# The mixer's pairs of column blocks: seven products in another order, partial sums taken from PSUM, and new constants for the recorder

## The chip, the cores and the metric

The kernel runs on one core of a Trainium2 chip. The metric is the device time of one execution in microseconds (us); for the kernel before it is 787.59 us, the median of 3 runs (787.1 to 787.76). A core has five engines that run side by side: TensorE multiplies matrices (the profile's PE, and PEld for its weight loads), VectorE (DVE) and ScalarE (ACT) do elementwise work and read the results of TensorE out of the memory called PSUM, GpSimd (POOL) does elementwise work in the other memory, SBUF, and SyncE (SP) issues most of the transfers.

## The reference

One step of a decoder layer for 512 prompt tokens and 8 x 4 sample tokens that share all weights (544 columns in all, D = 1024). Cut to what matters here:

```
h = rmsnorm(x, norm_mix);  z = h @ w_in            # the mixer's input: 28 blocks of 128 columns
aq, ak, av, hq, hf, hi, hg = split(z)              # attention q, k, v; HGRN q, forget gate, input, output gate
att = dilated_attention(aq, ak, av)                # also over cached keys and values for the samples
o   = hgrn2_recurrence(silu(hq), 1 - f, hi, log f) # f from hf; then norm, times silu(hg)
x  += concat(att, o) @ w_out
x  += cross_attention(rmsnorm(x), memory)          # memory keys and values from w_ck, w_cv
x  += (silu(conv3(u @ w_gate)) * (u @ w_up)) @ w_down,  u = rmsnorm(x)
```

All is float32. The kernel multiplies large matrices in a rounded float32 format in three passes: each operand is split into a high and a low part, and high x high, high x low and low x high are summed.

## The kernel before

Tokens lie along the free dimension (N = 544, two halves of HT = 272 columns), features along the 128 partitions. A block of 128 output features of the mixer is made either whole, by `proj_in` (8 feature tiles x 3 passes, in two cuts of 256 and 288 columns), or two blocks at once, by `proj_pair` (line 1198). The list `MIX` gives the order: h0, q0 to q3, k0, k1, then the pairs k2 with k3, v0 with v1, hf1 with hq1, hg1 with hv1 (the item `('H', 1)` makes two pairs), then the single blocks again. So `proj_pair` runs four times in a kernel. (The output projection, `wo_pair`, and the feed-forward part have pairs of their own, which the diff leaves as they are.)

A pair is Strassen's scheme in Winograd's form: the weights of two blocks are cut into A11, A12 (first block) and A21, A22 (second block), the tokens into B11, B21, B12, B22, and seven products replace eight. `take_pair` (line 861) makes the sums of weights S1 to S4, `make_blocks` the sums of tokens X, T, U, V. Each product is 12 matmuls (4 feature tiles x 3 passes) 272 columns wide. They gather in three PSUM banks: a and c come from the pool of two banks for main products ("dense"), d from the pool of five for everything else ("aux"). Bank a receives A11·B11, then S2·U, then S1·T, then S4·B22, each added onto what is there; after each of them a partial sum is read from the bank before the next product may be added.

In the kernel before the order of products is A11·B11 (a), S3·X (c), S2·U (a), A12·B21 (d), S1·T (a), S4·B22 (a), A22·V (c). ScalarE copies bank a three times: after A11·B11 into the first block's output, after S2·U and after S1·T into the two halves of an SBUF tile named `kept` (z and r). The second block's halves are then bank c minus r and bank c minus z, on VectorE (`difference`), and each half is multiplied by the row of normalisers r_mix, on VectorE too.

The order of all instructions is made by a recorder, the class `Tape` (its constants are at line 282). The kernel's functions don't issue instructions; they record steps with their reads and writes. Products under `tape.main()` form one chain whose order on TensorE is the order of recording. All else on TensorE (attention scores, HGRN blocks, the products with cached keys and values) is side work, which the recorder places between main products. It runs a model of the engines on the host, and what that model decides is the order in which each engine gets its instructions. On the chip the engines wait for each other by semaphores, so the order is fixed and the times are not. The rules that the constants set:

- Each step has a time at which it is due (`begin`), reckoned back from the steps that use it: a step that a main product needs is due `MARGIN` earlier still, and a step that nothing presses gets `SLACK` after it could start. A step on an engine other than TensorE may start up to `LEAD` ahead of its due time, unless a lead of its own is given.
- When TensorE is free and a main product is ready, a group of side work is opened if the ready side work sums to `BURST` us, or has waited for `PATIENCE` us, or is due; `NEAR` is what a change of the tile's shape counts in the choice of the next. When no main product is ready, side work runs as it comes.
- `FETCH` is the time from the asking for the next block of 256 of TensorE's instructions to its landing; side work that would run into a block not yet landed is held back. `ACTIVE` is the least share of busy time that TensorE must keep for side work to be let in.
- `EVEN` stretches the estimated times of the main chain.

In the profile nearly every instruction has line 726, the recorder's replay; so the tiles' names tell the work apart: `ps_ak`, `ps_ck`, `ps_dk` are the banks a, c, d of the first pair, `ps_av`, `ps_ahf`, `ps_ahg` bank a of the other three, `psd` and `psdo` products with cached keys and values, `psS`, `psT`, `psO` prompt attention, `psA`, `psB`, `psL`, `psin`, `psu`, `psU`, `pso` HGRN.

Of the kernel before, what the change touches and what calls it, by code (L numbers as in the profile page):

```python
# [12 lines left out]
AF = mybir.ActivationFunctionType  # L13
ALU = mybir.AluOpType
# [7 lines left out]
N = SEQ + NS  # L22
# [21 lines left out]
def ROWS_ON(nc):  # L44
    return nc.vector
# [9 lines left out]
HT = N // 2  # L55
# [218 lines left out]
class Tape:  # L274
# [4 lines left out]

    ROUNDS, EVEN = 2, 1.008
    BLOCK, AHEAD_OF, FETCH = 256, 63, 4.3
    SWITCH, NEAR = 0.16, 8.9
    SPELL, ACTIVE, IDLE, COLD = 3.4, 0.44, 0.45, 2.0
    BURST, PATIENCE, SLACK, LEAD, MARGIN = 2.05, 13.75, 14.4, 20.8, 1.3
    AHEAD = {"SP": 8, "ACT": 5, "DVE": 5, "POOL": 5, "PE": 8}

    def __init__(self, nc):
# [441 lines left out]
def tile_decoder_step(ctx: ExitStack, tc: tile.TileContext, xT, memT, kwT, vw, s0, conv_in, mkT, mv, vecs, cst,  # L731
                      w_first, w_in, w_out, w_cq, w_ck, w_cv, w_co, w_gate, w_up, w_down,
                      yT, kT_out, vT_out, st_out, conv_out, mkT_out, mv_out, ss_out):
    nc = tape = Tape(tc.nc)
# [9 lines left out]
    def A(name, shape=None, dt=F32):  # L744
        return tape.tile(act, shape or [128, FW], dt, tag="a", name=name, bufs=NA)
# [7 lines left out]
    def PD(name):  # L753
        return tape.tile(psum, [128, 512], F32, tag="dense", name=name, bufs=2)

    def PX(name):
        return tape.tile(psum, [128, 512], F32, tag="aux", name=name, bufs=5)
# [290 lines left out]
    r_mix, mix_acc = A("r_mix"), A("acc_mix")  # L1048
# [4 lines left out]
    first = [A(f"h{n}0") for n in "fqg"]  # L1053
# [109 lines left out]
    def proj_evac(out, scale, ps, n0, n):  # L1163
        if scale is None:
            nc.vector.tensor_tensor(out[:, n0:n0 + n], ps[:, :n], r_mix[:, n0:n0 + n], op=ALU.mult)
        else:
            nc.vector.scalar_tensor_tensor(out[:, n0:n0 + n], ps[:, :n], scale, r_mix[:, n0:n0 + n],
                                           op0=ALU.mult, op1=ALU.mult)
# [29 lines left out]
    def proj_pair(names):  # L1198

        name, outs = names[0], [A(n) for n in names]  # L1200
        w = ws.take_pair(name)
        a, c, d, kept = PD(f"ps_a{name}"), PD(f"ps_c{name}"), PX(f"ps_d{name}"), A(f"kept{name}")
        z, r = kept[:, :HT], kept[:, HT:N]

        def product(ps, wn, xn, first):
            with tape.main():
                for k in range(4):
                    (hi, lo), (xh, xl) = w[wn][k], mix_blocks[xn][k]
                    for i, (l, x_) in enumerate(((hi, xh), (hi, xl), (lo, xh))):
                        nc.tensor.matmul(ps[:, :HT], l, x_, start=first and k == 0 and i == 0, stop=k == 3 and i == 2,  # L1210
                                         skip_group_check=True)
            if wn not in ("S1", "S4", "A12"):
                sides.pump()

        def difference(c0, sub):
            out = outs[1][:, c0:c0 + HT]
            nc.vector.tensor_tensor(out, c[:, :HT], sub, op=ALU.subtract)
            ROWS_ON(nc).tensor_tensor(out, out, r_mix[:, c0:c0 + HT], op=ALU.mult)

        out = outs[0][:, :HT]  # L1220
        product(a, "A11", "B11", True)
        nc.scalar.copy(out, a[:, :HT])
        product(c, "S3", "X", True)
        product(a, "S2", "U", False)
        nc.scalar.copy(z, a[:, :HT])
        product(d, "A12", "B21", True)
        nc.vector.tensor_tensor(out, d[:, :HT], out, op=ALU.add)
        nc.vector.tensor_tensor(out, out, r_mix[:, :HT], op=ALU.mult)
        product(a, "S1", "T", False)
        nc.scalar.copy(r, a[:, :HT])  # L1230
        difference(HT, r)
        product(a, "S4", "B22", False)
        proj_evac(outs[0], None, a, HT, HT)
        product(c, "A22", "V", False)
        difference(0, z)
        return outs

    def proj_in(name, scale=None):
# [274 lines left out]
    mixed, outs = [None] * 8, [None] * 8  # L1513
# [199 lines left out]
    def each(kind, at, scale=None):  # L1713
        names = [f"{kind}{p}" for p in at]
        return proj_pair(names) if len(at) > 1 else [proj_in(names[0], scale)]
# [45 lines left out]
    def project_hgrn(what, h):  # L1761
        names = [f"h{n}{h}" for n in "fqg"] + [f"hv{h}"]
        if h == 0:
            f, q, gt, v = first + [proj_in(names[3])]
        elif what == "H":
            f, q, gt, v = proj_pair(names[:2]) + proj_pair(names[2:])
        else:
            f, q, gt, v = [proj_in(n) for n in names]
        hgrn(h, f, q, gt, v)
# [327 lines left out]
    hid, ups, ugs, whole, firsts, lows = {}, {}, {}, {}, {}, {}  # L2097
# [763 lines left out]
    while rest:  # L2861
        m, c = rest.pop(0)
# [81 lines left out]
```

## Time and profile before

| | |
|---|---|
| median of 3 runs | 787.59 us (787.1 to 787.76) |
| profiled execution | 786.92 us, of it 785.1 us span |
| PE busy | 774.4 us (99% of the span), 7411 matmuls |
| DVE busy | 688.9 us (88%) |
| ACT busy | 493.2 us (63%) |
| POOL busy | 216.1 us (28%) |
| mean granted TensorE clock | 0.998 |

The span runs from the first to the last instruction of the profiled execution; what its time has beyond the span lies around it. A row of the chain of waits is: start in us, duration in us, what ran (engine, tile, line, count). A row of a group of instructions is: line, engine, operation, out<-in, shapes, count | busy us, mean ns of one | idle time of the engine just before them and what ended it. A row of a stage is: the stretch, its length, then busy time and count of PE, PEld, DVE, ACT and POOL, the granted clock, the DMA engines' share and GB/s.

### The profile page before, as it was taken

To read this page: it belongs to the slowest core of one execution; us is meant where nothing else is said; L and a number is where in the kernel's file an instruction comes from. 1 tells how busy PE (TensorE), PEld (TensorE's weight loads), DVE (VectorE), ACT (ScalarE), POOL (GpSimd) and SP (SyncE) were. 2 spreads that over 40 slices of the span, in tenths; PEclk is the share of its full clock that TensorE was granted. 3 is DMA by queue.
4 is the path that set the end of the run, shared out by engine and by line. 5 is a ranking of instruction groups with operands and counts; after the bars stand their busy time and mean duration, and the time that the engine had idled before them with its cause. 6 is when DMAs were issued, how large, how long until landed. Compare 5 with 4: busy or idle time off the path is not lost.

```text
span 785.1 us, 19260 instructions
## 1 busy us (share of the span) xinstructions
PE 774.4 (99%) x7411; PEld 737.4 (94%) x7411; DVE 688.9 (88%) x1538; ACT 493.2 (63%) x1066; POOL 216.1 (28%) x298
## 2 busy tenths in 40 slices
PE   9999999999999999999999999999999999999996
PEld 8998879897899989999899999999999999999995
DVE  6899988588988989896779999999999998979983
ACT  7733467826559576574776677656665765668543
POOL 1131100031210431242234436522433242232122
PEclk9999999999999999999999999999999999999999
DMA  8745887697872776252663477887878968776303
GB/s 312 262 149 146 268 291 257 225 338 263 262 242 82 216 167 206 83 195 75 203 211 81 106 196 169 180 195 178 188 168 185 214 149 206 194 183 196 91 1 114
DMA packets 109116, 146.23 MB, mean 186 GB/s; under 512 B 7520, under 2 KB 74080, under 8 KB 109024
## 3 DMA queue, kind: packets, MB, share of 16 engines
q1 hardware_dynamic: 90992, 121.72, 47.6%
q0 software_dynamic: 17184, 22.55, 17.7%
q8 instruction: 58, 0.95, 0.5%
q10 hardware_dynamic: 848, 0.72, 0.3%
q14 instruction: 34, 0.28, 0.1%
HBM read 136.90 MB, written 8.07 MB: 185 GB/s over the span
## 4 chain that ended last, share of the span: by engine, by line
PE 95%; DVE 1%; ACT 1%; issue 1%; DMA 1%; SPq 0%; DVEq 0%
PE ps_ag L726 8%; PE ps_au L726 8%; PE ps_aw L726 5%; PE ps_cu L726 4%; PE ps_cg L726 4%; PE ps_q L726 3%; PE ps_wo L726 3%; PE ps_cq L726 3%; PE ps_dz L726 3%; PE ps_az L726 3%; PE ps_hv L726 2%; PE ps_cw L726 2%; PE ps_first L726 2%; PE ps_dg L726 2%; PE ps_du L726 2%; PE ps_ck L726 2%
## 5 line engine op out<-in xcount | busy, mean ns | idle before, releaser
L726 DVE TENSOR_TENSOR wl<-wr,wh 128x512 fp32r<-128x512 f32 x86 | 61.2, 735 | 1.5 <-ACT wh L726 1.5
L726 POOL TENSOR_TENSOR hG<-hG,hf 128x256 f32<-128x256 f32 (+1 forms) x28 | 25.5, 910 | 125.8 <-DVE hf L726 80.5
L726 ACT CAST wh<-wr 128x512 fp32r<-128x512 f32 x86 | 49.4, 616 | 5.2 <-DMA wr<-in_w_in 5.1
L726 POOL COPY last<-ug 128x2 f32<-128x2 f32 (+1 forms) x44 | 26.0, 636 | 87.4 <-DVE ug L726 80.0
L726 DVE SCALAR_TENSOR_TENSOR cv<-ug,vec,cv 128x560 f32<-128x560 f32 x44 | 35.1, 798 | 0.8 <-ACT cv L726 0.2
L726 POOL TENSOR_TENSOR acc_cx<-acc_cx,sq_cx 128x256 f32<-128x256 f32 (+1 forms) x14 | 13.9, 999 | 40.7 <-ACT sq_cx L726 40.4
L726 POOL COPY ug<-conv_state 128x16 f32<-128x16 f32 x22 | 23.6, 1138 | 0.0
L726 ACT ACTIVATE cv<-cv 128x560 f32<-128x560 f32 x22 | 14.8, 672 | 11.4 <-DVE cv L726 11.0
L726 ACT ACTIVATE cv<-ug,vec 128x560 f32<-128x560 f32 x22 | 18.9, 858 | 4.6 <-DVE ug L726 2.9
L697 POOL DMA_DIRECT2D S13w<-in_w_down x12 | 11.7, 978 | 36.3 <-DMA S13w<-in_w_down 9.0
L726 ACT ACTIVATE P<-P,mx 128x128 f32<-128x128 f32 (+3 forms) x32 | 17.6, 553 | 3.0 <-DVE mx L726 3.0
L726 PE MATMUL ps_co<-coh,wh 128*128 128x256 f32 (+1 forms) x64 | 19.2, 300 | 0.0
L726 POOL TENSOR_TENSOR acc_final<-acc_final,sq_final 128x256 f32<-128x256 f32 (+1 forms) x10 | 9.3, 942 | 35.0 <-ACT sq_final L726 18.3
L726 PE MATMUL ps_co<-col,wh 128*128 128x256 f32 (+1 forms) x64 | 18.4, 288 | 0.0
L726 PE MATMUL ps_co<-coh,wl 128*128 128x256 f32 (+1 forms) x64 | 18.4, 288 | 0.0
L697 POOL DMA_DIRECT2D A22w_0l<-in_w_down x6 | 12.2, 2042 | 18.2 <-DMA S13w<-in_w_down 7.1
L726 POOL TENSOR_TENSOR acc_ux<-acc_ux,sq_ux 128x256 f32<-128x256 f32 (+1 forms) x13 | 11.3, 873 | 21.0 <-ACT sq_ux L726 21.0
L726 POOL MEMSET hG<- 128x544 f32 x4 | 2.2, 551 | 51.7 <-PE psO L726 44.1
L726 ACT COPY keptg<-ps_ag 128x272 f32<-128x272 f32 x20 | 7.7, 385 | 13.3 <-PE ps_ag L726 13.2
L726 DVE TENSOR_TENSOR xr<-xr,ps_aw 128x272 f32<-128x272 f32 x36 | 15.5, 430 | 0.4 <-PE ps_aw L726 0.2
L726 POOL MEMSET ug<- 128x2 f32 x22 | 15.7, 763 | 0.0
L726 PE MATMUL psd<-st,qbd_win 128*32 128x224 f32 x256 | 15.7, 357 | 0.0
(3466 smaller groups left out, 3841.1 us busy)
## 6 DMA issues: line engine op xcount, KB each, us to landing
st<-in_kwT SPq DMA_DIRECT2D x32, 448.0 KB, 6.1
st<-in_vw SPq DMA_DIRECT2D x28, 512.0 KB, 6.2
wr<-in_w_in SPq DMA_DIRECT2D x25, 512.0 KB, 6.4
wrg<-in_w_gate SPq DMA_DIRECT2D x10, 512.0 KB, 6.0
wru<-in_w_up SPq DMA_DIRECT2D x10, 512.0 KB, 5.5
st<-in_mkT SPq DMA_DIRECT2D x8, 512.0 KB, 6.4
S13w<-in_w_down SPq DMA_DIRECT2D x24, 128.0 KB, 5.1
A1w<-in_w_down SPq DMA_DIRECT2D x12, 256.0 KB, 4.2
```

What stands on the lines that cost most here:

```text
L697: return tape.put(engine, lambda: call(*args, **kw), outs, ins, 0.1, 0.3, size)
L726: return tape.put(engine, lambda: call(*args, **kw), outs, ins, length, lag, size, port, codes, work, mode)
```

## The change

In `proj_pair` A22·V moves ahead of S4·B22, so the order is A11·B11 (a), S3·X (c), S2·U (a), A12·B21 (d), S1·T (a), A22·V (c), S4·B22 (a). The tile `kept` goes. ScalarE now copies bank c after S3·X into the second block's right half, and bank a, times -1, after S2·U into its left half. VectorE then takes right minus bank a after S1·T, and left plus bank c after A22·V, in place (`whole`), and multiplies by r_mix as before. The side work's generators are moved on once after the same four products as before (`sides.pump()`), so the last of these calls now comes ahead of S4·B22.

Nine of the recorder's constants get new values; its code stays.

```diff
-    ROUNDS, EVEN = 2, 1.008
-    BLOCK, AHEAD_OF, FETCH = 256, 63, 4.3
-    SWITCH, NEAR = 0.16, 8.9
-    SPELL, ACTIVE, IDLE, COLD = 3.4, 0.44, 0.45, 2.0
-    BURST, PATIENCE, SLACK, LEAD, MARGIN = 2.05, 13.75, 14.4, 20.8, 1.3
+    ROUNDS, EVEN = 2, 0.993
+    BLOCK, AHEAD_OF, FETCH = 256, 63, 5.2
+    SWITCH, NEAR = 0.16, 6.85
+    SPELL, ACTIVE, IDLE, COLD = 3.4, 0.48, 0.45, 2.0
+    BURST, PATIENCE, SLACK, LEAD, MARGIN = 1.4, 4.45, 15.85, 30.05, 3.5
...
-        a, c, d, kept = PD(f"ps_a{name}"), PD(f"ps_c{name}"), PX(f"ps_d{name}"), A(f"kept{name}")
-        z, r = kept[:, :HT], kept[:, HT:N]
+        a, c, d = PD(f"ps_a{name}"), PD(f"ps_c{name}"), PX(f"ps_d{name}")
...
-        def difference(c0, sub):
-            out = outs[1][:, c0:c0 + HT]
-            nc.vector.tensor_tensor(out, c[:, :HT], sub, op=ALU.subtract)
+        def whole(out, bank, op):
+            nc.vector.tensor_tensor(out, out, bank[:, :HT], op=op)
+            c0 = HT * (out is right)
             ROWS_ON(nc).tensor_tensor(out, out, r_mix[:, c0:c0 + HT], op=ALU.mult)
 
-        out = outs[0][:, :HT]
+        first, (left, right) = outs[0][:, :HT], (outs[1][:, :HT], outs[1][:, HT:N])
         product(a, "A11", "B11", True)
-        nc.scalar.copy(out, a[:, :HT])
+        nc.scalar.copy(first, a[:, :HT])
         product(c, "S3", "X", True)
+        nc.scalar.copy(right, c[:, :HT])
         product(a, "S2", "U", False)
-        nc.scalar.copy(z, a[:, :HT])
+        nc.scalar.activation(left, a[:, :HT], AF.Copy, scale=-1.0)
         product(d, "A12", "B21", True)
-        nc.vector.tensor_tensor(out, d[:, :HT], out, op=ALU.add)
-        nc.vector.tensor_tensor(out, out, r_mix[:, :HT], op=ALU.mult)
+        whole(first, d, ALU.add)
         product(a, "S1", "T", False)
-        nc.scalar.copy(r, a[:, :HT])
-        difference(HT, r)
+        whole(right, a, ALU.subtract)
+        product(c, "A22", "V", False)
+        whole(left, c, ALU.add)
         product(a, "S4", "B22", False)
         proj_evac(outs[0], None, a, HT, HT)
-        product(c, "A22", "V", False)
-        difference(0, z)
         return outs
```

## The prediction

> **What bounds the kernel now.** I read the page's head and busy shares first, then its chain of work that ended last, then the stages, then what the PE waits for.
>
> ```profile
> span 785.1 us, 19260 instructions
> PE 774.4 (99%) x7411; PEld 737.4 (94%) x7411; DVE 688.9 (88%) x1538; ACT 493.2 (63%) x1066; POOL 216.1 (28%) x298
> PE 95%; DVE 1%; ACT 1%; issue 1%; DMA 1%; SPq 0%; DVEq 0%
> ```
>
> The PE is busy for 99% of the span and is 95% of the chain. The busy share hides what a matmul costs, so the stages (columns: length, busy time and count for each engine, clock, DMA) say where there is room at all:
>
> ```profile
> 75.00:160.00 85.00, 84.53 (x894) 74.04 (x894) 67.06 (x188) 54.95 (x123) 5.16 (x7) 1.00 0.78 259
> 160.00:300.00 140.00, 139.13 (x1853) 122.50 (x1852) 124.65 (x328) 85.20 (x200) 35.73 (x44) 1.00 0.72 220
> 300.00:425.00 125.00, 124.54 (x1058) 119.79 (x1057) 104.41 (x215) 79.25 (x197) 38.38 (x45) 1.00 0.49 155
> 425.00:725.00 300.00, 300.00 (x2391) 299.99 (x2391) 287.87 (x591) 201.07 (x405) 110.76 (x164) 1.00 0.76 178
> ```
>
> From 425 to 725 us (the feed-forward part) the PE has no idle time, at a granted clock of 1.00; 300 us for 2391 matmuls is 125 ns each, as fast as a product of twelve gets anywhere (1.51 us, below). No new order wins there. From 75 to 425 us the PE is idle for 0.47 + 0.87 + 0.46 = 1.8 us. The waits of the PE name them (who waits, for whom, us, times, longest):
>
> ```profile
> PE ps_first L726 <- DVE zero L726: 1.1, 1, 1.1
> PE ps_ak L726 <- ACT keptk L726: 0.5, 1, 0.5
> PE psdo L726 <- ACT dom L726: 0.5, 1, 0.5
> PE ps_g L726 <- DVE xr L726: 0.5, 1, 0.5
> PE psL L726 <- ACT hAT L726: 0.3, 1, 0.3
> ```
>
> The first is the start, written in a fixed order that the diff leaves alone. The second is one of the changed pairs. So the question is small: a wait of half a microsecond, and how the side products (attention, HGRN, cached keys) are placed between the main ones, which the recorder decides.
>
> **The change part by part.** In each of the four pairs (k2 with k3, v0 with v1, hf1 with hq1, hg1 with hv1) the old order ends S1·T on bank a, S4·B22 on bank a, A22·V on bank c. S4·B22 may not start until a copy of bank a is done, and no main product lies between. The chain of waits around that place in the first pair (start, us, what):
>
> ```profile
> 89.27 1.51 PE ps_ak L726 x12
> 90.78 0.02 issue
> 90.80 0.40 ACT keptk L726
> 91.20 0.04 issue
> 91.24 1.79 PE ps_ak L726 x12
> ```
>
> The PE stands for 0.02 + 0.40 + 0.04 = 0.46 us, and the product behind it takes 1.79 instead of 1.51, 0.28 more. The new order puts A22·V, on the other bank, into that place: it takes 1.51 us and covers the release. First term: 0.46 + 0.28 = 0.74 us won.
>
> In the other three pairs the recorder filled the same hole with side products (second pair; for comparison a group of sixteen; third; fourth):
>
> ```profile
> 106.22 0.52 PE psd L726 x8
> 106.74 1.74 PE ps_av L726 x12
> ...
> 100.64 0.89 PE psd L726 x16
> ...
> 125.01 1.31 PE psT L726 x12
> ...
> 131.07 0.52 PE psd L726 x8
> 131.59 0.45 PE ps_ahf L726 x2
> ...
> 150.54 2.30 PE psdo L726 x40
> 152.84 1.71 PE ps_ahg L726 x12
> 154.55 1.51 PE ps_chg L726 x12
> ```
>
> Eight psd take 0.52 us, sixteen 0.89: eight more cost 0.37, so entering side work costs 0.52 - 0.37 = 0.15 fixed, and the main product behind it takes 1.71 instead of 1.51, another 0.20. An opening, then, costs 0.35 us beside its work. The group of eight at 106.22 stands alone only because nothing else could run; with A22·V ready it can join a later group. Second term: 0.35 us. The 2.30 us group is large enough to be opened for itself, and so is the third pair's, from 125.01 to 131.59; I count nothing for them (between nothing and 0.35 each, kept in the range).
>
> What the new order adds: bank a is now freed for S4·B22 by VectorE's subtraction (right minus a), where ScalarE's copy did it. The rows of the two operations between 75 and 160 us, and of a VectorE subtraction that reads SBUF alone:
>
> ```profile
> L726 ACT COPY keptk<-ps_ak 128x272 f32<-128x272 f32 x2 | 0.8, 388 | 1.1 <-PE ps_ak L726 1.1
> L726 DVE TENSOR_TENSOR k<-ps_ck,keptk 128x272 f32<-128x272 f32 x2 | 0.9, 432 | 0.0
> L726 DVE TENSOR_TENSOR xT<-x 128x272 f32<-128x272 f32 x4 | 1.6, 428 | 0.0
> ```
>
> Old and new have the same number of operations in a pair, three on ScalarE and seven on VectorE, all 272 wide (four of the seven read PSUM in both). The scaled copy (scale -1) has no row of its own at this width; I take the copy's 388 ns, with nothing and double that as the ends, off the path either way. So the sum of engine work is nothing, and what matters is whether VectorE comes in time. In the first pair its queue behind the end of S1·T (90.78) looked like this:
>
> ```profile
> 91.10 0.69 DVE L726 TENSOR_TENSOR S1l_v<-S_v,S1h_v 128x512 fp32r<-128x512 f32 x1
> 91.70 0.43 DVE L726 TENSOR_TENSOR k<-ps_ck,keptk 128x272 f32<-128x272 f32 x1
> ```
>
> Two 0.69 us weight splits stood before it; it ended at 92.13, 1.35 us after S1·T. With the 0.04 us of release that is 1.39, and A22·V covers 1.51. The cover holds, by 0.12 us. One more split ahead of the subtraction would cost 0.69 - 0.12 = 0.57 and the 0.28 behind a wait. I take nothing, with 0.85 us a pair as the bad end.
>
> The Trainium skill, Advanced Engine Details and Errata, The Read-Write Bubble, says that ScalarE is the engine close to PSUM and VectorE the one close to SBUF, which speaks against freeing a bank by VectorE. The trace bears it out by very little: 432 ns from PSUM against 428 from SBUF, and 388 on ScalarE, which by that rule would be 0.04 us a pair under a cover of 1.51.
>
> The end of a pair: before, bank a was free one product ahead of bank c; now c is free one product ahead of a. The next main tile finds one free bank with 1.51 us of cover in both, as at 156 us in the old trace, where the next tile follows the pair's last product without a gap. The old tile of kept halves goes, which frees one of 71 SBUF tiles: nothing, since no wait of the PE names a missing tile. In the last pass, one VectorE operation instead of two follows the last product: 0.43 us earlier, hidden under the next tile's products.
>
> **The constants** shift every step that isn't written in a fixed order. Later landing of instruction blocks (4.3 to 5.2 us) keeps side products away from block boundaries. What the profile shows of blocks (a DMA queue: packets, MB, share):
>
> ```profile
> q8 instruction: 58, 0.95, 0.5%
> ```
>
> 58 blocks of 16 KB feed the PE, and every idle stretch of the PE after the start is named above with an engine as its end, none with a block. There is nothing to win from this edit by itself. The Trainium skill, Runtime: NRT & Kernel Launch, Instruction fetch mechanics, has the next block fetched while the present one runs and the crossing mostly hidden; the trace agrees for the PE.
>
> A smaller least size for a group (2.05 to 1.4 us) and less patience (13.75 to 4.45 us) make for more openings; a longer lead (20.8 to 30.05) and an earlier due time (margin 1.3 to 3.5 us) bring work forward, which makes groups larger and takes away waits. I count 24 groups with narrow tiles in the chain from the first to the last of these rows:
>
> ```profile
> 46.67 0.75 PE psB L726 x59
> ...
> 289.16 1.64 PE pso L726 x14
> ```
>
> 24 openings at 0.35 are 8.4 us. If groups shrank with the least size there would be 24 x 2.05 / 1.4 = 35, 3.9 us more; if the work that comes forward let one in four be merged, 2.1 us less. The two pull against each other and I take nothing. The remaining waits (psdo on dom 0.5, ps_g on xr 0.5, psL on hAT 0.3, together 1.3 us) hang on one operation that came late by less than the 2.2 us by which due times move forward. The one on xr is VectorE itself standing before its work:
>
> ```profile
> 418.55 1.49 issue
> 420.05 0.45 DVE xr L726
> 420.50 0.04 issue
> ```
>
> 1.49 us in which VectorE waited for nothing that the profile shows; such a thing moves when its instructions move. I take half of the 1.3, 0.6 us, with nothing and 1.3 as the ends.
>
> **The sum.** 0.74 + 0.35 + 0.6 = 1.7 us. The profiled execution took 786.92 (span 785.1 and 1.8 around it); 786.92 - 1.7 = 785.2. The median of the runs is 787.59, 0.67 above it, and moves alike: 787.59 - 1.7 = 785.9. The three runs lie between 787.1 and 787.76; about 0.2%, 1.6 us, is what a measurement of this kernel can tell from no change, so this forecast lies at that edge.
>
> **The rivals.** First, the wins go back where they came from: the two certain terms hold (1.1 us) but new waits of the size of the old ones appear elsewhere, or VectorE is late in one pair (0.85) or three groups more are opened (1.05). For it: 24 groups are placed anew, and each wait in the list is a matter of tenths. Against it: the holes in the pairs were in all four. Time: 787.59 - 1.1 + 0.85 = 787.3, and 786.5 if nothing is given back. That the block constant does nothing at all (no stall to remove) belongs here.
>
> Second, slower: more openings. Place: between 46 and 291 us. Mechanism: a group starts at 1.4 us of ready side work or after 4.45 us, so work that filled one group is split in two. Price 0.35 us each; from 5 more openings the 1.7 us are gone, and from about 10 the kernel is slower by over 0.2%. With the full 11 worked out above and only the two certain terms: 787.59 - 1.1 + 3.9 = 790.4; with 11 and the full sum, 789.8. For it: the groups of 0.52 and 0.89 us above show that small groups do get opened and what they cost. Against it: most groups are longer than 2 us, where neither limit decides, and earlier work makes them longer. I take 789.8 as its time.
>
> Third, VectorE is late in all four pairs: 4 x 0.85 = 3.4 us against 1.7 won, 789.3. It decides from a subtraction that starts over 1.0 us after S1·T. Against it: the worst queue that I found in the old trace still fits.
>
> **How the numbers follow.** The forecast, 785.9, and better: 0.43; in it lie merged groups, down to 787.59 - 1.1 - 1.3 - 1.4 (four openings fewer) = 783.8. Wins that go back or no effect, 786.1 to 789.1: 0.36. Slower by openings 0.15, by VectorE 0.06. So faster 0.43, same 0.36, slower 0.21. The range for 8 in 10 runs from 783.8 to 789.4; below it and above it I leave about one in ten each. The likeliest case's own range is 783.8 to 786.5.
>
> **What would show it.** Right: no PE wait on a copy or a subtraction between S1·T and S4·B22 in the four pairs, A22·V directly behind S1·T or behind a large group; the subtraction from bank a ending less than 1.5 us after S1·T; no group of eight psd alone in a pair; 24 groups or fewer. Wrong: PE waits on the tiles k, v, hq or hv from VectorE (the third rival); 30 groups or more, or many of under 1 us (the second); waits of the PE that sum to 1.8 us again at other places (the first). The feed-forward part must still be 125 ns a matmul without idle time: if it isn't, all of this was argued about the wrong stage.

## The result and the profile after

The kernel after takes 785.19 us (median of 10 runs, 784.64 to 785.92) where the kernel before took 787.11 beside it (10 runs, 786.69 to 787.76): a ratio of 0.9975, with a 95% interval of 0.9966 to 0.9985. That is 1.9 us less, against 1.7 forecast.

The page's head, busy shares and chain of the kernel after:

```profile
span 783.4 us, 19292 instructions
PE 774.4 (99%) x7411; PEld 737.6 (94%) x7411; DVE 687.7 (88%) x1538; ACT 495.5 (63%) x1066; POOL 216.9 (28%) x298
PE 98%; DMA 1%; DVE 0%; SPq 0%; ACT 0%; issue 0%; DVEq 0%
```

The PE is busy for 774.4 us in both kernels; the span is 1.7 us shorter. So the gain is idle time of the PE. The stages of the kernel after say where:

```profile
75.00:160.00 85.00, 84.96 (x901) 74.56 (x900) 67.06 (x186) 52.88 (x118) 6.59 (x7) 1.00 0.79 269
160.00:300.00 140.00, 139.98 (x1851) 123.36 (x1850) 124.42 (x333) 87.95 (x203) 35.42 (x44) 1.00 0.72 214
300.00:425.00 125.00, 125.00 (x1067) 120.66 (x1066) 106.48 (x217) 81.00 (x201) 37.28 (x43) 1.00 0.50 157
425.00:725.00 300.00, 300.00 (x2391) 299.84 (x2390) 286.86 (x588) 200.34 (x402) 114.35 (x168) 1.00 0.75 178
```

Length less busy time is 0.04 + 0.02 + 0.00 = 0.06 us in the first three stages, where it was 0.47 + 0.87 + 0.46 = 1.80: 1.74 us less. The feed-forward stage is as it was, 2391 matmuls in 300 us. What the PE still waits for in the whole kernel after (who, for whom, us, times, longest):

```profile
PE ps_first L726 <- DVE zero L726: 1.1, 1, 1.1
PE ps_first L726 <- ACT xm0h L726: 0.3, 1, 0.3
```

Both lie in the start, which the diff doesn't touch. The four waits that were to be had (k2's pair 0.5, dom 0.5, xr 0.5, hAT 0.3) are gone, and none of their size has come in their place. (A gap of 0.04 us ahead of the first pair's S3·X is new.)

The last row of the first pair in the kernel before, and then the chain of waits of the kernel after in the first, second and fourth pair:

```profile
93.03 1.51 PE ps_ck L726 x12
...
82.42 0.04 issue
82.46 1.78 PE ps_ck L726 x12
...
89.60 1.50 PE ps_ak L726 x12
91.10 1.51 PE ps_ck L726 x12
92.61 1.51 PE ps_ak L726 x12
...
103.21 1.70 PE ps_av L726 x12
104.91 1.51 PE ps_cv L726 x12
106.42 1.51 PE ps_av L726 x12
...
150.49 1.70 PE ps_ahg L726 x12
152.19 1.51 PE ps_chg L726 x12
153.71 1.51 PE ps_ahg L726 x12
```

In these and in the third pair, A22·V (the row on bank c) stands between S1·T and S4·B22, and S4·B22 follows it without a gap at the pace of an undisturbed product, 1.51 us. In the first pair the stretch from the start of S1·T to the end of the pair was 5.27 us (89.27 to 94.54) and is now 4.52 (89.60 to 94.12), 0.75 less. The lone group of eight psd in the second pair is gone. The first two of VectorE's four subtractions that free bank a, from its timeline:

```profile
91.79 0.43 DVE L726 TENSOR_TENSOR k<-k,ps_ak 128x272 f32<-128x272 f32 x1
...
105.22 0.43 DVE L726 TENSOR_TENSOR v<-v,ps_av 128x272 f32<-128x272 f32 x1
```

They end 1.12 and 0.74 us after S1·T (at 91.10 and 104.91), those of the other two pairs 0.48 us after it. The first is the latest; with the release of 0.04 it uses 1.16 of the 1.51 us that A22·V covers.

Where the time went by place: the single block behind the pairs (`ps_hf`) begins at 155.41 instead of 155.90, the output projection (`ps_wo`) at 300.21 instead of 301.35, the feed-forward part (`ps_g`) at 418.72 instead of 420.54, and the PE's last matmul at 775.54 instead of 777.40. So 1.14 us come from the mixer, another 0.68 from the cross attention and its end, and nothing after it.

### The profile page after: what moved, and what is told of

It is laid out like the page before. It is cut to its first block, busy times and chain, and to the rows that moved or that the text cites. A ratio compares the mean times of both kernels' runs of the same rounds, so it can differ in the third digit from the quotient of the medians.

```text
span 783.4 us, 19292 instructions
## 1 busy us (share of the span) xinstructions
PE 774.4 (99%) x7411; PEld 737.6 (94%) x7411; DVE 687.7 (88%) x1538; ACT 495.5 (63%) x1066; POOL 216.9 (28%) x298
## 4 chain that ended last, share of the span: by engine, by line
PE 98%; DMA 1%; DVE 0%; SPq 0%; ACT 0%; issue 0%; DVEq 0%
PE ps_ag L726 8%; PE ps_au L726 8%; PE ps_aw L726 5%; PE ps_cg L726 4%; PE ps_cu L726 4%; PE ps_q L726 3%; PE ps_co L726 3%; PE ps_wo L726 3%; PE ps_cq L726 3%; PE ps_dz L726 3%; PE ps_az L726 3%; PE ps_hv L726 2%; PE ps_cw L726 2%; PE ps_first L726 2%; PE ps_dg L726 2%; PE ps_du L726 2%
## 5 line engine op out<-in xcount | busy, mean ns | idle before, releaser
L726 POOL COPY last<-ug 128x2 f32<-128x2 f32 (+1 forms) x44 | 32.7, 778 | 62.9 <-DVE ug L726 61.1
L726 POOL COPY ug<-conv_state 128x16 f32<-128x16 f32 x22 | 20.4, 1027 | 0.0
L726 DVE CUSTOM_DVE_ANT_0 P<-psS,bias 128x128 f32<-128x128 f32 (+3 forms) x32 | 14.1, 486 | 2.1 <-PE psS L726 2.1
```

The lines of the kernel that those rows point to most:

```text
L726: return tape.put(engine, lambda: call(*args, **kw), outs, ins, length, lag, size, port, codes, work, mode)
```

## The experiments

All times are medians of runs beside runs of the kernel before on the same chip (787.14 for the first four, 787.38 for the next four, 787.31 for the last four), five rounds each. "Groups" counts the stretches of side work between two main products that hold matmuls with narrow tiles, in the whole kernel, my count over the PE's matmuls in the trace: 27 before (the 24 of the prediction and 3 in the cross attention) and 27 after.

My theory was that the new order closes the hole between S1·T and S4·B22 and that the constants then matter little. The rival was that each half of the change is worth nothing alone: the recorder lays all of the kernel anew for any edit, and the nine constants fit one code.

### The halves of the change

**New order and sums, old constants.** The kernel after with the nine old values.

> The new order of products and the new sums with the nine old constants. Theory A (the holes between S1*T and S4*B22 are what the order removes; the constants take away other waits): about 1.1 us less than the kernel before (786.0 against 787.1), no PE wait inside a pair, the waits on dom, hAT and xr free to stay. Theory B (any new placing by the constants made the gain, the order is worth nothing): 787.1, within 0.3 us of the kernel before.

Measured: 793.69 us, ratio 1.0078 (1.0063 to 1.0093). Its largest waits of the PE behind the start:

```profile
PE ps_wo L726 <- DVE om3l L726: 1.0, 1, 1.0
PE ps_wo L726 <- ACT om3h L726: 0.8, 1, 0.8
PE ps_g L726 <- DVE xr L726: 0.5, 1, 0.5
```

No wait is left in the pairs, as in the kernel after. But there are 31 groups, and the mixer's last output is late for the output projection: the tiles `ps_wo` hold the PE for 27.86 us instead of 24.07. Of these 3.79 us, 1.73 are the two waits (0.75 and 0.98). The rest lies in slower matmuls behind them, at a lower clock (third column from the end), where the kernels before and after have 1.00:

```profile
305.00:310.00 5.00, 3.27 (x20) 2.86 (x19) 4.90 (x13) 3.60 (x8) 0.00 (x0) 0.86 0.94 297
310.00:315.00 5.00, 5.00 (x37) 5.00 (x36) 5.00 (x9) 1.58 (x3) 0.00 (x0) 0.80 0.52 177
```

Four of the five executions have a mean granted clock of 0.994 or 0.995 and take 793.56 to 794.66 us; the fifth has 0.998 and takes 791.12. So the new order and sums without the new constants are 0.8% slower, and by that one execution some 2.6 of the 6.5 us hang on the clock.

**Old order and copies, new constants.** The kernel before with the nine new values.

> The old order with its kept copies, with the nine new constants. Theory A: 0.6 to 0.8 us less than the kernel before (786.4), the waits on dom, hAT and xr gone, but a wait on a copy or a small group of side work between S1*T and S4*B22 in each pair. Theory B: the whole gain, 785.2.

Measured: 789.83 us, ratio 1.0036 (1.0023 to 1.0048), 30 groups. The chain in its first pair:

```profile
91.20 0.02 issue
91.23 0.39 ACT keptk L726
...
91.67 1.78 PE ps_ak L726 x12
```

It is the hole of before, with its 1.78 us product behind it, and the second pair now has the same: 0.5 us on `keptv`. The waits on dom, xr and hAT are gone here too, with the old order.

**The new sums alone**, S4·B22 still ahead of A22·V, old constants:

```diff
         product(a, "S1", "T", False)
         whole(right, a, ALU.subtract)
-        product(c, "A22", "V", False)
-        whole(left, c, ALU.add)
         product(a, "S4", "B22", False)
         proj_evac(outs[0], None, a, HT, HT)
+        product(c, "A22", "V", False)
+        whole(left, c, ALU.add)
```

> The new sums taken from PSUM in the old order of products, so that S4*B22 follows S1*T on bank a and waits for VectorE's subtraction from it; old constants. Theory A (the cover by A22*V is what counts): no faster than the kernel before, and slower by 0.1 to 0.9 us in each pair whose hole isn't filled with side work, so 787.1 to 789; the PE waits on VectorE in at least one pair, and takes 1.7 us or more for the product behind it. If the sums themselves were the gain (the freed SBUF tile, the missing copies of bank a): 786.0.

Measured: 788.88 us, ratio 1.0023 (1.0014 to 1.0032), 28 groups. Its wait in the first pair:

```profile
PE ps_ak L726 <- DVE k L726: 0.7, 1, 0.7
```

VectorE frees bank a later than ScalarE did (the PE waits 0.7 against 0.5 us) when nothing covers it.

**The new order alone**, with the old tile `kept` and the old copies, old constants:

```diff
         product(a, "S1", "T", False)
         nc.scalar.copy(r, a[:, :HT])
         difference(HT, r)
+        product(c, "A22", "V", False)
+        difference(0, z)
         product(a, "S4", "B22", False)
         proj_evac(outs[0], None, a, HT, HT)
-        product(c, "A22", "V", False)
-        difference(0, z)
```

> The new order of products with the old kept copies: A22*V may start only when ScalarE has copied bank a after S1*T and VectorE has then taken the difference out of bank c. Old constants. Theory A: the hole only moves, from ahead of S4*B22 to ahead of A22*V, and grows from one operation (0.4 us) to two (0.9 us): 787.1 to 789, with side work or a wait ahead of A22*V in every pair. If the order alone were the gain: 786.0.

Measured: 792.20 us, ratio 1.0064 (1.0052 to 1.0077), 36 groups; no wait in the pairs, new ones elsewhere (0.9 us in the feed-forward part, 0.8 on dmx, 0.6 on ho).

What follows: all four parts are slower alone, by 0.2 to 0.8%, and together they are faster by 0.25%. Their effects don't add, as the rival says. What the recorder does with the rest of the kernel (1 to 9 groups more) outweighs the hole itself. To price the hole, the placing must be held still.

### The order on a placing that is held still

**The new order on the placing of before.** The recorder lays the code of before with the old constants. On its finished list S4·B22 and A22·V are exchanged in all four pairs, with the VectorE steps behind them, and the copies and sums are replaced by the new ones; all other steps keep their place, save those that then have to wait for a moved one.

```diff
-        for s in best[1]:
+        for s in self.exchanged(best[1]):
...
+        for name in ("k2", "v0", "hf1", "hg1"):
+            for one, two in (("S4", "A22"), ("first", "low")):
+                i, j = done.index(get[name, one]), done.index(get[name, two])
+                done[i], done[j] = done[j], done[i]
```

> The placing of every side product is that of the kernel before, step for step (the recorder plans the old code with the old constants); only then, in the four pairs, S4*B22 and A22*V change places, the copies and sums become the new ones, and a few VectorE steps follow. So this is the change of order and sums with no new placing. Theory A (the holes cost time by themselves): 0.74 us less from the first pair alone, as the prediction has it, and up to some 1.9 if the other pairs give something too: 785.2 to 786.4, with no PE wait on the first pair's copy. Theory B (the placing alone counts): 787.1, within 0.3.

Measured: 786.94 us, ratio 0.9998 (0.9989 to 1.0007). The chain in the first pair:

```profile
89.80 1.49 PE ps_ak L759 x12
91.29 1.51 PE ps_ck L759 x12
```

and its waits of the PE, those of the start left out:

```profile
PE ps_g L759 <- DVE xr L759: 0.5, 1, 0.5
PE psdo L759 <- ACT dom L759: 0.5, 1, 0.5
PE psL L759 <- ACT hAT L759: 0.3, 1, 0.3
...
PE psA L759 <- issue: 0.2, 1, 0.2
```

The hole is gone: the tiles `ps_ak` hold the PE for 6.29 us instead of 6.86, 0.57 less. The waits on xr, dom and hAT stand where they stood. The last row is a new one (0.25 us, behind an instruction block), and the score products of one group run in another order and cost 0.65 more. So the order does in the pair what was said of it. In the whole run the 0.65 and the 0.25 take it back, and no gain can be told from nothing: the interval goes from 0.9 us less to 0.6 more.

**The old order on the placing of after**, twice: the same exchange on the list of the kernel after. In the first of the two, some steps read the second block's left half ahead of its sum, so that part of the result is of other numbers; in the second, those steps are held until the sum is made.

```diff
+            for one, two in (("A22", "S4"), ("low", "first")):
...
+            s4.deps.discard(a22)
+            a22.deps.add(s4)
```

> The placing of the kernel after, step for step, with S4*B22 moved back ahead of A22*V in the four pairs (the new sums stay, so S4*B22 waits for VectorE's subtraction from bank a, uncovered). Theory A: 0.7 us or more in every pair in which A22*V stood right behind S1*T, so 1 to 3 us more than the kernel after: 786.2 to 788.2, with PE waits on VectorE ahead of S4*B22. Theory B: 785.2.

> The placing of the kernel after, with S4*B22 moved back ahead of A22*V in the four pairs, as in e6, and now every step that reads the second block's left half held until its sum is made (in e6 some steps that read that half came before it, so part of its result was of other numbers). Theory A: as e6, about 3 to 4 us more than the kernel after, with the PE waiting for VectorE ahead of S4*B22 in three pairs: 788.2 to 789.2. If e6's loss came from the steps that ran out of turn: 785.2 to 786.

Measured: 789.18 us, ratio 1.0025 (1.0014 to 1.0035), for the first; 790.21 us, ratio 1.0043 (1.0030 to 1.0057), for the second. The chain of the second in the first pair:

```profile
91.86 0.36 DVE k L760
92.22 0.04 issue
92.26 1.77 PE ps_ak L760 x12
```

and its waits of the PE:

```profile
PE ps_ak L760 <- DVE k L760: 1.2, 1, 1.2
...
PE pst_hv L760 <- DVE hv L760: 1.0, 1, 1.0
PE ps_av L760 <- DVE v L760: 0.8, 1, 0.8
PE ps_ahg L760 <- DVE hv L760: 0.5, 1, 0.5
```

Three of the four pairs wait ahead of S4·B22. (`pst_hv` is a side product that stands right behind the fourth pair and reads the half that the old order finishes last.) The first pair's 1.2 us are the 1.16 that the kernel after hides under A22·V. The PE's last matmul starts 4.84 us later than in the kernel after (780.38 against 775.54), and the tiles of bank a in the first, second and fourth pair and of bank c in the fourth hold it for 1.34 + 1.04 + 0.79 + 1.20 = 4.37 us more. So in this placing the new order is worth 4 us (the first run) to 5 us (the second): the recorder, which no longer had to fill the holes with side work, has put that work elsewhere, and the kernel after can't do without the cover.

### The constants, one group at a time

**The old landing time of blocks**: the kernel after with `FETCH` 4.3 instead of 5.2.

> The kernel after with FETCH back at 4.3. If TensorE's instruction blocks really land late and the constant keeps side work out of their way: PE waits for nothing that the profile names ('issue') inside groups of side products, some tenths of a us each, 786 to 788. Theory A and B both: no such wait; only another placing, which the recorder itself puts 0.7 us later than that of the kernel after (its planned end 776.5 against 775.8), so 785.9.

Measured: 787.39 us, ratio 1.0000 (0.9991 to 1.0008), 29 groups. The chain at its one new wait:

```profile
279.50 0.80 PE psO L726 x11
280.30 1.05 issue
281.35 0.32 PE psO L726
```

The PE stands for 1.05 us in the middle of a group of prompt attention, with no engine that it waits for. The packet of an instruction block on queue q8 ran from 279.06 to 280.04; the PE goes on at 281.35, 1.31 after its end. The span is 2.4 us longer than that of the kernel after; 1.05 of it is this wait, and 1.46 are busy time of the PE (775.84 against 774.38), with 96 changes of the tile's shape instead of 89.

**The old limits for a group**: the kernel after with `BURST` 2.05 and `PATIENCE` 13.75.

> The kernel after with BURST and PATIENCE back at 2.05 and 13.75. The prediction's second rival says that the new limits make for more openings, so the old ones would make it faster, by up to 3.9 us: 781 to 785. Theory B (each set of constants is one draw of a placing, and the recorder's planned end tells which is good): planned end 778.7 against 775.8, 2.9 us more: 788.1.

Measured: 789.70 us, ratio 1.0033 (1.0020 to 1.0045). There are 29 groups, not fewer than 27, though a group must now be larger or wait longer. The PE stands here too, by the same sign behind a block, with `FETCH` at 5.2:

```profile
169.10 0.85 issue
169.95 0.27 PE psB L726 x5
```

The block's packet ran from 167.53 to 168.65; the PE goes on 1.30 us after its end. The busy time of the PE is 3.2 us longer than in the kernel after (777.60), with 103 changes of shape.

**Far smaller limits**: `BURST` 0.3 and `PATIENCE` 0.5.

> The kernel after with BURST 0.3 and PATIENCE 0.5, so that side work starts as soon as there is any. The recorder then opens 37 groups with narrow tiles instead of 27. At the prediction's price of 0.35 us an opening: 3.5 us more than the kernel after, 788.7; the planned end (779.81 against 775.81) says 4.0 more, 789.2. If an opening costs nothing: 785.2.

Measured: 790.53 us, ratio 1.0040 (1.0027 to 1.0052). Its stage from 160 to 300 us:

```profile
160.00:300.00 140.00, 140.00 (x1842) 121.19 (x1841) 124.57 (x326) 88.14 (x204) 36.82 (x44) 1.00 0.74 219
```

The PE is never idle here and waits for 0.2 us in all behind the start, and yet the span is 788.4, 5.0 us above that of the kernel after. There are 37 groups instead of 27, and 118 changes of the tile's shape instead of 89: 0.5 us for each group more, or 0.17 for each change. This is the run that prices them best, since hardly any wait stands beside it. The price of a change holds in kind in the other sets of constants: 1.46 us more busy time for 7 changes more with the old landing time, 3.2 for 14 with the old limits, 2.1 for 8 with the old lead below, 0.2 to 0.3 each. The price of a group doesn't: these three have only 2 or 3 groups more, 0.7 to 1.6 us for each. Nor do changes of shape account for all: the neighbouring set below, with one change more, is busy 1.1 us longer, beside three waits.

**The old lead and due times**: `SLACK`, `LEAD`, `MARGIN` at 14.4, 20.8, 1.3.

> The kernel after with SLACK, LEAD and MARGIN back at 14.4, 20.8 and 1.3. The prediction's third term says that the earlier due times take away the waits on dom, hAT and xr: with the old ones these come back, 0.6 to 1.3 us more, 785.8 to 786.5. Theory B: planned end 778.14, 2.3 us more, 787.5, whatever waits there are.

Measured: 787.71 us, ratio 1.0006 (0.9997 to 1.0015), 30 groups, 97 changes of shape. Its one wait after the start:

```profile
PE ps_au L726 <- DVE S4u2l L726: 0.5, 1, 0.5
```

The waits on dom, xr and hAT have not come back. So the earlier due times are not needed to keep them away.

**A neighbouring set**: `EVEN` 0.976 and `SLACK` 15.79, for which the recorder reckons almost the same end as for the values of the kernel after.

> The kernel after with EVEN 0.976 and SLACK 15.79 in place of 0.993 and 15.85: another placing whose planned end, 775.87, is within 0.1 us of the kernel after's (775.81). Theory B (the planned end tells): 785.3, within 0.5. If the set of constants of the kernel after is good by something that the planned end doesn't see: 786.5 or more, with waits of the PE that the plan doesn't have.

Measured: 786.78 us, ratio 0.9992 (0.9984 to 1.0001), 30 groups. Three waits that the kernel after doesn't have: 0.5 us at 22.4 us (the normalisers, on acc_mix), 0.5 on hAT and 0.3 on a tile `keptg` of the feed-forward part.

The recorder's own reckoning of the PE's end, on the host, beside the measured medians (us):

```
                            reckoned   measured
kernel after                 775.81     785.19
neighbouring set             775.87     786.78
kernel before                775.60     787.11
landing 4.3                  776.51     787.39
old lead and due times       778.14     787.71
new sums alone               777.91     788.88
old limits                   778.73     789.70
new constants alone          778.36     789.83
far smaller limits           779.81     790.53
new order alone              782.91     792.20
new order and sums           783.96     793.69
```

It follows the measured order to within about 1 us (measured less reckoned: 9.3 to 11.5). In the last two rows 4.0 and 2.0 us of the reckoned end are what the recorder adds where it expects a lower clock. The trace shows the lower clock in the very last (above), and none for the new order alone (mean granted clock 0.998), so that row agrees in part by chance. This is how the constants can be read: each kernel has the constants that fit its own code. With each of the six other sets that were run, the code of after is reckoned later than with its own and is slower, up to 8.5 us (785.19 against 793.69); with the new set the code of before is slower too. The kernel after is not better by the reckoning (775.81 against 775.60), and the gain of 1.9 us is no larger than the spread of measured less reckoned, so the reckoning could not foretell it. What the kernel after has over the kernel before on the chip is that it lacks waits that the reckoning doesn't see.

## Why the prediction was right

The time is right: 1.7 us less forecast, 1.9 measured. Its terms were less good than their sum, and that they met the result is in part luck. By the stages, 1.74 us of idle time went and the PE's busy time stayed; the forecast had 0.46 + 0.6 = 1.06 us of idle time and 0.28 + 0.35 = 0.63 of cheaper products. The 0.7 us that the idle time gave beyond the forecast made up for the products, which gave nothing in the sum. That the new placing as a whole cost nothing was a bet too: in the six other placings that other constants gave the new code, it cost 1.6 to 8.5 us.

- **The first pair's wait (0.74 forecast).** The mechanism is right: the wait is gone in the kernel after and with the order alone on the placing of before, and it comes back when the order is taken back, on the placing of after or under the new constants. So is the size at that place: 0.75 us less from S1·T to the end of the pair (0.60 on the placing of before, where S4·B22 takes 1.67). But the new placing gave part of it back inside the pair. S3·X, which had followed a group of side work and taken 1.70, now waits for VectorE's last operation on block k1 (81.96 to 82.41): the gap is only 0.04 us, but the product takes 1.78. And the group stands ahead of A12·B21, which takes 1.70 instead of 1.49. So `ps_ak` holds the PE for only 0.46 us less. A gap of 0.04 us makes the product behind it as slow as one of 0.46 did (1.79).
- **The lone group in the second pair (0.35).** It is gone; `ps_av` holds the PE for 0.27 us less. But a group went from one place and came at another: 27 and 27. The cheaper products of these two terms show in their own tiles and nowhere in the sum; the changes of shape rose from 84 to 89, at 0.17 each 0.85 us, which would account for it.
- **The other waits (0.6, half of 1.3).** All of the 1.3 us went. The half was a guess, and its reason, that the earlier due time "takes away waits", isn't borne out: with the old due times and lead they stay away, while under the new constants they are gone with the old order as well. What the runs show in its place is only that another placing moves them. For one of them, on xr, the trace suggests a cause, in the last section. For dom and hAT it stays open.
- **The number of openings, at nothing.** Right, 24 and 24 up to 291 us. Its price was too low: 0.35 against 0.5 with the far smaller limits, and more in the other sets, where the changes of shape and not the groups tell the cost. The second rival's premise, that the smaller limits make for more groups, did not hold: with the old limits the new code has 29, not fewer. Only limits far below both do what it said.
- **VectorE's cover.** Right: 1.16 of 1.51 us used, 1.39 forecast, and the third rival stays out. The bad end of 0.85 a pair was reckoned for one more split ahead of the subtraction, with the cover in place, and no run shows that case. With no cover at all the first pair waits 1.2 us and its tiles cost 1.34.
- **The block constant.** "There is nothing to win from this edit by itself" was wrong in time: with the old value all of the gain is lost (1.0000). It was read from the trace of before, where no block makes the PE wait. How the value does it is not shown, since it changes the whole placing: the wait of 1.05 us is one part, more changes of shape are another. Nor is it shown that 5.2 keeps such waits away, for with 5.2 the old limits still give one of 0.85, and the kernel before has none with 4.3. What can be drawn from it is that a new placing may bring a stall that the old trace lacks.
- **The first rival**, that the wins go back elsewhere, did not come about in the kernel after. But every other placing of the new code that was run ends 1.6 to 8.5 us above it, with waits or openings that the kernel after doesn't have.

What stays open: whether the order has a worth of its own in the time of a whole run (0.57 us in its pair, and nothing that can be told apart in the run), and which of the nine constants removes the waits on dom and hAT: 1.3 of the 1.74 us of idle time won have no cause that a run shows. The neighbouring set is 1.6 us slower with 0.06 us more by the reckoning; its three waits come to 1.2 of that, and what the rest is was not separated.

## What to carry to other kernels

Where several products add into one bank and each partial sum must be read out, put a product on another bank between the reader and the next writer: a 0.4 us copy then needs no cover of side work, and work that had been used to fill the hole may go where it is cheaper. Where a planner lays out the whole kernel, compare an edit only with constants fitted to each version, and price it by exchanging steps on a finished plan, with an eye on the other steps that the exchange moves; each half of this change alone was 0.2 to 0.8% slower. Look at the waits on instruction blocks in runs of many small matmuls even when the present trace has none.

## What the runs showed of the hardware

**Instruction blocks seem to stop TensorE.** Five runs have stops without an engine that is waited for, in dense groups of small matmuls: 1.05 us (old landing time), 0.85 (old limits), 0.25 (new order on the placing of before), 0.25 and 0.22 (new order and sums) and 0.10 (new sums alone). In all six the PE goes on between 1.25 and 1.58 us after the end of a block's packet on queue q8; no run changed the blocks alone. In the third the packet ran from 45.94 to 47.16 and the PE went on at 48.74, 1.58 after; in the kernel before the packet of the same block ended at 46.67 and nothing stopped. The Trainium skill, Runtime: NRT & Kernel Launch, Instruction fetch mechanics, calls the crossing mostly hidden. In the kernels before and after it is hidden at every block; in these five it seems not to be, at one or two of the blocks.

**Changes of the tile's shape cost busy time, not idle time.** The Trainium skill, TensorEngine Tiling (Array Packing), Key Properties, says that a change of the tiling mode drains TensorE, and gives no price. Here, with the far smaller limits, the PE is busy 4.9 us longer (779.31 against 774.38) with 29 changes of shape more, 0.17 each, and 0.2 to 0.3 in three other sets; the busy share doesn't show it.

**A lower clock stood behind two waits.** With the new order and sums the PE stands for 0.75 and 0.98 us between 305.76 and 307.88, and the granted clock is 0.86 from 305 to 310 us and 0.80 from 310 to 315, then 1.00 again. No other run has a stretch of 10 us between 30 and 770 us under 0.985, though single waits of up to 1.17 us occur. No run was made to separate the waits from the clock.

**VectorE held beside GpSimd, perhaps.** The wait on xr that the prediction left as "nothing that the profile shows" has an instruction under it. The timeline of the kernel before, VectorE's operation and then GpSimd's:

```profile
416.72 0.47 DVE L726 SCALAR_TENSOR_TENSOR B<-xr,vec,r_ux 128x256 f32<-128x256 f32 x1
...
418.41 1.72 DVE L726 SCALAR_TENSOR_TENSOR B<-xr,vec,r_ux 128x256 f32<-128x256 f32 x1
...
417.84 1.15 POOL L697 DMA_DIRECT2D S3g<-in_w_gate  x1
418.45 1.38 POOL L726 TENSOR_TENSOR acc_ux<-acc_ux,sq_ux 128x288 f32<-128x288 f32 x1
```

The same operation takes 0.47 us and then 1.72, beside a GpSimd sum that takes 1.38 and that follows the issue of a weight transfer without a pause. In the kernel after three of these operations take 1.94 us together, the longest 1.03 (first row); the sums and issues on GpSimd are further apart, as the other rows show:

```profile
412.94 1.94 DVE L726 SCALAR_TENSOR_TENSOR B<-xr,vec,r_ux 128x256 f32<-128x256 f32 x3
...
413.64 0.95 POOL L726 TENSOR_TENSOR acc_ux<-acc_ux,sq_ux 128x288 f32<-128x288 f32 x1 [0.41 <-ACT sq_ux L726]
414.54 0.86 POOL L697 DMA_DIRECT2D S3g<-in_w_gate  x1
```

The four kernels in which the PE waits on xr for 0.5 us (before, the new order and sums, the new sums alone, the new order on the placing of before) are those that have this operation at 1.71 or 1.72 us; elsewhere the longest ones take 0.67 to 1.35. No run was made to separate the two engines, so this is a cause that the traces suggest and that was not tested.
